# Mixture-of-experts passes of a two-layer block: the next pass's first gate and up products issued before the down products

## The chip, the cores and the metric

The kernel runs on one core of one Trainium2 chip. The metric is device time in microseconds (us) of one execution, the median of three runs. TensorE (PE in the profile) multiplies, with its weight loads shown apart (PEld); VectorE (DVE) and ScalarE (ACT) read its results out of PSUM; SyncE (SP) issues the loads of weights.

## The reference

Two blocks of two layers each work on 256 tokens; the second block has 256 context tokens beside them in its first layer. The change lies in the mixture of experts at the end of each layer of the second block, `hier_moe`. Each token goes to two of 32 experts, and for every expert

```
h_e = rows of h that were sent to expert e
y_e = (silu(h_e @ w_gate[e]) * (h_e @ w_up[e])) @ w_down[e]      # 1024 -> 512 -> 1024, f32
out[token] += weight[token, e] * y_e
```

All 32 experts' weights (6 MiB each in f32) are read once per layer. Layer 0 has 512 tokens, layer 1 has 256.

## The kernel before

Each expert has 64 slots for rows. Two experts make a pass: their products lie side by side in the 128 rows of a PSUM bank, the first in rows 0 to 63 and the second in rows 64 to 127. So a layer has 16 passes. Layer 0 has a 17th (`extra`), for one expert with more than 64 rows, which has 128 slots and half the weights. Two passes make a quad of four experts.

A pass has these parts (line numbers of the kernel before):

- `wload` (L1561): SP loads one tile of 1 MiB, [128, 4, 512], into a buffer of one of two pools, `ring` (4 buffers) for every third load and `ring2` for the others. A pass of two experts takes 12 tiles: four for gate and up with the first half of the model width (`kh` 0), four for the second half (`kh` 1), four for down. A buffer comes free when PE has read it.
- gate and up (L1640): 32 matmuls in f32 with 64 columns each, in pairs, one for each expert. In the trace every such f32 matmul is two instructions, so a pass has 64 rows of them. They write the banks `psg` and `psu`.
- `hidden` (L1527 to L1530): tanh on ACT, then two operations on DVE, which end in `eac`.
- `turned` (L1538, L1539): PE turns `eac` with four transposes, ACT copies them out as `eaT`.
- down (L1667): 16 matmuls, 32 rows in the trace, then `split_y` (L1547, L1548), which makes the pair `yh`, `yl`.
- `gather` (L1586, L1587): PE multiplies the tokens with a one-hot matrix (`goh`, made by DVE at L1568), which gives the four experts' rows `xg`. In layer 0 it has four units of 16 instructions for each quad.
- `combine` (L1517, L1518): the way back to the tokens with the transposed one-hot matrix `est`; in layer 0 eight units of four instructions for each quad. DVE reads each unit out (L1520) and adds it to `x` (L1521).
- `scatter_of` (L1602, L1609): four transposes and eight small products, which make `est` and the gate weights `egs`.

`gather` and `combine` are generators. The loop asks them for a unit at fixed places in the program; a scheduler then orders each engine's instructions by what they depend on, so on PE single instructions of one part stand between those of another. PE runs them in the order in which they stand. PSUM has four banks for the products (`acc`) and three for `gather`, `combine`, `turned` and `scatter_of` together (`aux`).

Of the kernel before, what the change touches and what calls it, by code (L numbers as in the profile page):

```python
# [1 line left out]

# [1 line left out]

# [7 lines left out]
F32 = mybir.dt.float32  # L12
F32R = mybir.dt.float32r
BF = mybir.dt.bfloat16
# [1117 lines left out]
        lin_a4(g, oh, ol, w2d, 8, [(512 * c, 512)], (range(half), range(half, len(xt))), ev, before)  # L1132


def open_ring2(g, l):
    g.ring2 = g.moe_st.enter_context(g.tc.tile_pool(name=f"ring2{l}", bufs=(6, 9)[l], side="right"))


def mixer_ab(g, xt):
# [194 lines left out]
def moe(g, l, xt):  # L1334
# [3 lines left out]
    with ExitStack() as st:  # L1338
# [212 lines left out]
        with ExitStack() as s1:  # L1551
# [4 lines left out]
            def wload(name, e, half):  # L1556

                src = h[name][l, e:e + 1] if isinstance(e, int) else h[name][l, ds(e, 1)]
                t = (g.ring2 if loads[0] % 3 else g.ring).tile([P, 4, 512], F32, name="wraw", tag="wraw")
                loads[0] += 1  # L1560
                nc.sync.dma_start(t.rearrange("p k n -> p (k n)"),  # L1561
                                  src.rearrange("e (p k) n -> p (e k n)", p=P)[:, 2048 * half:2048 * half + 2048])
                return t

            def onehot(q, dt):
                oh = pe.tile([P, nt, 4, CAP], dt, name="goh", tag=f"goh{dt}", bufs=2)
                for t in range(nt):
                    nc.vector.tensor_tensor(oh[:, t], posm[:, t, 4 * q:4 * q + 4, None].to_broadcast([P, 4, CAP]),  # L1568
                                            g.iota[:, None, :CAP].to_broadcast([P, 4, CAP]), op=OP.is_equal)
                return oh  # L1570

            def onehot_first(px, dt):
                oh = pe.tile([P, nt, 4, CAP], dt, name="goh", tag=f"goh{dt}", bufs=2)
                for t in range(nt):
                    nc.vector.tensor_scalar(oh[:, t, :2].rearrange("p e c -> p (e c)"), g.iota, px[:, t:t + 1], None, op0=OP.is_equal)
                return oh

            def gather(oh, xg, n=4):
                w = n * CAP
                for fp in range(4):  # L1580
                    ps = g.aux.tile([P, 2, 256], F32, name="auxps", tag="aux")
                    for j in range(2):
                        f = 2 * fp + j
                        for t in range(nt):
                            r = oh[:, t, :n].rearrange("p e c -> p (e c)")
                            nc.tensor.matmul(ps[:, j, :w], hh[:, t, f * P:(f + 1) * P], r, start=(t == 0), stop=False)  # L1586
                            nc.tensor.matmul(ps[:, j, :w], hl[:, t, f * P:(f + 1) * P], r, start=False, stop=(t == nt - 1))  # L1587
                    if fp % 2:
                        nc.scalar.copy(xg[:, 2 * fp:2 * fp + 2, :w], ps[:, :, :w])
                    else:  # L1590
                        nc.vector.tensor_copy(xg[:, 2 * fp:2 * fp + 2, :w], ps[:, :, :w])
                    yield

            def step(units, n):
                for _ in range(n):
                    next(units, None)

            def scatter_of(obp, gates3):

                psb = g.aux.tile([P, nt * P], BF, name="auxpb", tag="aux")  # L1600
                for t in range(nt):
                    nc.tensor.transpose(psb[:, t * P:(t + 1) * P], obp[t], g.identb)  # L1602
                stt = pe.tile([P, nt * P], F32R, name="est", tag="est", bufs=3)
# [12 lines left out]
            xg = pe.tile([P, 8, 4 * CAP], F32, name="xg")  # L1616
            oh = onehot(0, F32R)
            start = gather(oh, xg)
            comb, parts = iter(()), []
            npass = NEXP // 2  # L1620
            first = None
            for pr_ in range(npass + extra):
                q, hp = pr_ // 2, pr_ % 2
                if pr_ < npass:
                    ex = [(slice(64 * e, 64 * e + 64), slice((2 * hp + e) * CAP, (2 * hp + e + 1) * CAP), 2 * pr_ + e) for e in range(2)]
                else:
                    ex = [(slice(0, P), slice(0, P), nc.values_load(tabE0[0:1, 0:1], engines=(mybir.EngineType.SP,), min_val=0, max_val=NEXP - 1))]
                psg = g.acc.tile([P, 512], F32, name="accps", tag="acc")
                psu = g.acc.tile([P, 512], F32, name="accps", tag="acc")
                for kh in range(2):  # L1630
                    step(start, 2)
                    if pr_ == 0 and kh == 0:
                        gates()
                        ob = onehot(0, BF)
                    for nm, pp in (("moe_w_gate", psg), ("moe_w_up", psu)):
                        w = [wload(nm, e, kh) for _, _, e in ex]
                        for k in range(4):
                            K = 4 * kh + k
                            for wt, (rows, cols, _) in zip(w, ex):
                                nc.tensor.matmul(pp[rows], xg[:, K, cols], wt[:, k], start=(K == 0), stop=(K == 7))  # L1640
                        if kh == 0 and pp is psg:
                            if pr_ < npass:
                                obp = [ob[:, t, 2 * hp:2 * hp + 2].rearrange("p e c -> p (e c)") for t in range(nt)]
                                stt, gs = scatter_of(obp, [lambda t, e=e: G3[:, t, e] for _, _, e in ex])
                            else:
                                obp = [ob[:, t, :2].rearrange("p e c -> p (e c)") for t in range(nt)]
                                stt, gs = scatter_of(obp, [lambda t: first[1][:, t]])
                        if hp == 0 and (nt == 4 or pp is psu):
                            step(comb, 2)
                ac = hidden(pe, psg, psu, gs)  # L1650
                turn = iter(())
                if hp == 1 and pr_ + 1 < npass:
                    turn = gather(oh, xg)
                elif pr_ + 1 == npass and extra:
                    turn = gather(oh, xg, 2)
                step(comb, 2 * nt)
                step(turn, 2)
                aT = turned(pe, ac)
                step(turn, 1)
                psd = [g.acc.tile([P, 512], F32, name="accps", tag="acc") for _ in range(2)]  # L1660
                for half in range(2):
                    w = [wload("moe_w_down", e, half) for _, _, e in ex]
                    for kk in range(2):
                        k = 2 * half + kk
                        for c in range(2):
                            for wt, (rows, _, _) in zip(w, ex):
                                nc.tensor.matmul(psd[c][rows], aT[:, k, rows], wt[:, 2 * kk + c], start=(k == 0), stop=(k == 3))  # L1667
                    step(turn, 1)
                parts.append((stt, *split_y(pe, psd, 2)))
                if hp == 1 or pr_ + 2 >= npass + extra:  # L1670
                    for _ in comb:
                        pass
                    comb = combine(pe, parts)
                    parts = []
                if pr_ == 0:
                    first = overflow_table(pe)
                if hp == 0 and pr_ + 2 < npass:
                    oh, ob_next = onehot(q + 1, F32R), onehot(q + 1, BF)
                elif hp == 0 and extra:
                    oh, ob_next = onehot_first(first[0], F32R), onehot_first(first[0], BF)  # L1680
                elif hp == 1:
                    ob = ob_next
            for _ in comb:
                pass

# [150 lines left out]
```

## Time and profile before

| | |
|---|---|
| median of 3 runs | 2850.63 us (2847.06 to 2854.13) |
| the profiled execution | 2851.21 us, span 2849.4 us |
| PE busy | 2679.5 us, 94% |
| PEld, DVE, ACT busy | 1848.9, 1542.7, 1023.0 us |
| bytes read | 690.80 MB, 243 GB/s over the span |
| expert weights read | 390 loads, 1 MiB each |
| layer 0's passes | from 1530.62 to 2099.40 us |
| layer 1's passes | from 2364.79 to 2830.58 us |

PE's busy time is the union of its matmuls' modelled times, so a busy PE can still have matmuls that follow each other more slowly than they could. The start of one row against the start of the next is the better measure, and it is used below.

### The profile page before, as it was taken

The numbers are of one execution on the slowest core, as the hardware profiler recorded it, in microseconds if no ns is written. First come the engines' busy times: TensorE is split into PE (matmuls) and PEld (weight loads), VectorE is DVE, ScalarE is ACT, GpSimd is POOL, SyncE is SP. The second block draws the span as 40 slices with busy tenths as digits, with TensorE's granted clock in tenths as the row PEclk, the third lists the DMA queues.
The fourth block names the chain that finished last, engine by engine and source line by source line (L and its number), as shares of the span: only waits on it lengthen the run. The fifth ranks groups of instructions, "written<-read, shape, count | busy, mean of one in ns | idle before, by whom it ended". The sixth has DMA issues, their size and how long they took to land. (4 is left out here: it accounts for less than half of the span.)

```text
span 2849.4 us, 39299 instructions
## 1 busy us (share of the span) xinstructions
PE 2679.5 (94%) x15773; PEld 1848.9 (65%) x15773; DVE 1542.7 (54%) x2886; ACT 1023.0 (36%) x1809; POOL 131.0 (5%) x172
## 2 busy tenths in 40 slices
PE   7999999999999999979998999999979998999997
PEld 5989889978899989766565444444458554433332
DVE  6767768857677678565755333332263555222223
ACT  4556546545575456343741110100022441111111
POOL 0000000000000000021011000000000330000000
PEclk9999999999999999989997999999989899999999
DMA  6544466664454576642155999999933357999996
GB/s 222 184 148 161 145 231 212 220 228 157 159 175 142 184 266 207 200 151 74 33 216 211 391 360 368 368 369 369 368 125 132 102 211 297 420 420 420 420 420 265
DMA packets 207434, 694.56 MB, mean 244 GB/s; under 512 B 18160, under 2 KB 67760, under 8 KB 151184
## 3 DMA queue, kind: packets, MB, share of 16 engines
q1 hardware_dynamic: 201424, 674.18, 63.4%
q0 software_dynamic: 5824, 17.82, 1.9%
q8 instruction: 126, 2.06, 0.3%
q14 instruction: 60, 0.49, 0.0%
HBM read 690.80 MB, written 1.15 MB: 243 GB/s over the span
## 5 line engine op out<-in xcount | busy, mean ns | idle before, releaser
L159 DVE TENSOR_TENSOR wlo<-wraw,whi 128x1024 fp32r<-128x1024 f32 (+1 forms) x406 | 484.9, 1200 | 221.7 <-ACT whi L158 211.5
L158 ACT CAST whi<-wraw 128x1024 fp32r<-128x1024 f32 (+1 forms) x406 | 418.0, 1035 | 394.2 <-PE accps L245 192.7
L1640 PE MATMUL accps<-wraw,xg 128*64 128x512 f32 x2080 | 506.2, 595 | 0.0
L1640 PEld LDWEIGHTS accps<-wraw,xg 128*64 128x64 f32 x2080 | 160.1, 137 | 289.8 <-issue 287.4
L1667 PE MATMUL accps<-wraw,eaT 128*64 128x512 f32 (+1 forms) x1040 | 276.9, 600 | 3.0 <-ACT eaT L1539 3.0
L244 PE MATMUL accps<-xh,whi 128*128 128x256 f32 x896 | 258.1, 288 | 0.0
L246 PE MATMUL accps<-xh,wlo 128*128 128x256 f32 x896 | 255.6, 285 | 0.0
L245 PE MATMUL accps<-xl,whi 128*128 128x256 f32 x896 | 255.3, 285 | 0.0
L244 PE MATMUL accps<-fxh,whi 128*128 128x256 f32 x704 | 200.5, 285 | 0.5 <-ACT whi L158 0.4
L246 PE MATMUL accps<-fxh,wlo 128*128 128x256 f32 x704 | 199.5, 284 | 0.6 <-DVE wlo L159 0.5
L245 PE MATMUL accps<-fxl,whi 128*128 128x256 f32 x704 | 199.6, 284 | 0.0
L244 PEld LDWEIGHTS accps<-xh,whi 128*128 128x128 f32 x896 | 170.3, 190 | 7.7 <-issue 7.4
L1667 PEld LDWEIGHTS accps<-wraw,eaT 128*64 128x64 f32 (+1 forms) x1040 | 82.3, 137 | 138.6 <-issue 125.7
L1548 DVE TENSOR_TENSOR yl<-accps,yh 128x512 fp32r<-128x512 f32 x66 | 45.5, 691 | 232.8 <-ACT yh L1547 232.6
L245 PEld LDWEIGHTS accps<-xl,whi 128*128 128x128 f32 x896 | 170.1, 190 | 1.2 <-issue 1.0
L246 PEld LDWEIGHTS accps<-xh,wlo 128*128 128x128 f32 x896 | 170.2, 190 | 1.1 <-issue 1.0
L244 PEld LDWEIGHTS accps<-fxh,whi 128*128 128x128 f32 x704 | 135.6, 193 | 6.2 <-issue 5.0
L246 PEld LDWEIGHTS accps<-fxh,wlo 128*128 128x128 f32 x704 | 135.3, 192 | 1.1 <-DVE wlo L159 1.1
L245 PEld LDWEIGHTS accps<-fxl,whi 128*128 128x128 f32 x704 | 135.6, 193 | 0.0
L1527 ACT ACTIVATE eth<-accps 128x512 f32<-128x512 f32 x33 | 19.7, 597 | 321.5 <-PE accps L1640 321.5
L1547 ACT CAST yh<-accps 128x512 fp32r<-128x512 f32 x66 | 38.7, 586 | 216.6 <-PE accps L1667 216.6
L1586 PE MATMUL auxps<-goh,hh 128*128 128x256 f32 (+1 forms) x416 | 109.7, 300 | 3.0 <-issue 3.0
(496 smaller groups left out, 5123.5 us busy)
## 6 DMA issues: line engine op xcount, KB each, us to landing
wraw<-in_moe_w_gate SPq DMA_DIRECT2D x130, 1024.0 KB, 11.4
wraw<-in_moe_w_up SPq DMA_DIRECT2D x130, 1024.0 KB, 12.7
wraw<-in_moe_w_down SPq DMA_DIRECT2D x130, 1024.0 KB, 11.8
wraw<-in_w_in SPq DMA_DIRECT2D x72, 1024.0 KB, 5.0
wraw<-in_w_ada SPq DMA_DIRECT2D x48, 1024.0 KB, 4.9
wraw<-in_ffn_w_up SPq DMA_DIRECT2D x88, 512.0 KB, 5.1
wraw<-in_ffn_w_down SPq DMA_DIRECT2D x20, 1024.0 KB, 5.2
wraw<-in_w_proj_ssd SPq DMA_DIRECT2D x16, 1024.0 KB, 5.1
```

What stands on the lines that cost most here:

```text
L158: nc.scalar.copy(hi[:, :jj, :n], t[:, j:j + jj, :n])
L159: nc.vector.tensor_tensor(lo[:, :jj, :n], t[:, j:j + jj, :n], hi[:, :jj, :n].bitcast(F32), op=OP.subtract)
L244: nc.tensor.matmul(o, wh, a, start=(K == 0 and f % per == 0), stop=False, skip_group_check=True)
L245: nc.tensor.matmul(o, wh, b, start=False, stop=False, skip_group_check=True)
L246: nc.tensor.matmul(o, wl, a, start=False, stop=last, skip_group_check=True)
L1527: nc.scalar.activation(th, psg, AF.Tanh, scale=0.5)
L1547: nc.scalar.copy(yh[:, sl], psd[c])
L1548: nc.vector.tensor_tensor(yl[:, sl], psd[c], yh[:, sl].bitcast(F32), op=OP.subtract)
L1586: nc.tensor.matmul(ps[:, j, :w], hh[:, t, f * P:(f + 1) * P], r, start=(t == 0), stop=False)
L1640: nc.tensor.matmul(pp[rows], xg[:, K, cols], wt[:, k], start=(K == 0), stop=(K == 7))
L1667: nc.tensor.matmul(psd[c][rows], aT[:, k, rows], wt[:, 2 * kk + c], start=(k == 0), stop=(k == 3))
```

## The change

The loop over passes is written anew. Pass p+1's gate and up products with the first half of the width come first, then pass p's `turned`, then one block with up to four units of `combine` and two of `gather` (layer 0), the scatter of pass p+1, then pass p's down products (into the banks that held its gate and up), and last pass p+1's second half of gate and up and its `hidden`. `in_order` chains all PE instructions of the loop in the order of the program text, without a semaphore. `xg` becomes two tiles, one for each half of the width. The one-hot matrices have one buffer instead of two, `est` five instead of three, `yh` and `yl` three instead of two. `ring2` of layer 0 has 5 buffers instead of 6, and loads go to the two pools in proportion to their sizes.

```diff
+@contextmanager
+def in_order(g):
+    tc = g.tc
+    cur = g.nc.cur_bb
+    n = len(cur.bb.instructions)
+    yield
...
+        if k >= n and prev is not None:
+            tc.add_manual_dep(i, prev.name, mybir.DependencyInfo(mybir.DependencyClass.NoSync, mybir.DependencyReason.DATA),
+                              reason="in_order")
+        prev = i
 def open_ring2(g, l):
-    g.ring2 = g.moe_st.enter_context(g.tc.tile_pool(name=f"ring2{l}", bufs=(6, 9)[l], side="right"))
+    g.ring2 = g.moe_st.enter_context(g.tc.tile_pool(name=f"ring2{l}", bufs=(5, 9)[l], side="right"))
+    g.nring2 = (5, 9)[l]
...
-                t = (g.ring2 if loads[0] % 3 else g.ring).tile([P, 4, 512], F32, name="wraw", tag="wraw")
+                t = (g.ring if 4 * loads[0] % (4 + g.nring2) < 4 else g.ring2).tile([P, 4, 512], F32, name="wraw", tag="wraw")
...
+            def gate_up(p, kh):
+                if not kh:
+                    exs[p] = experts(p)
+                    banks[p] = [g.acc.tile([P, 512], F32, name="accps", tag="acc") for _ in range(2)]
+                for nm, pp in zip(("moe_w_gate", "moe_w_up"), banks[p]):
+                    w = [wload(nm, e, kh) for _, _, e in exs[p]]
+                    for k in range(4):
+                        K = 4 * kh + k
+                        for wt, (rows, cols, _) in zip(w, exs[p]):
+                            nc.tensor.matmul(pp[rows], xg[kh][:, k, cols], wt[:, k], start=(K == 0), stop=(K == 7))
+                if kh:
+                    acs[p] = hidden(pe, *banks[p], gsc[p][1])
...
+            gate_up(0, 0)
+            step(turn, 2)
+            scatter(0)
+            oh = onehot(1, F32R)
+            gate_up(0, 1)
+            first = overflow_table(pe)
+            comb, parts, turn = iter(()), [], iter(())
+            with in_order(g):
+                for p in range(passes):
+                    q, hp = p // 2, p % 2
+                    more = p + 1 < passes
+                    if more:
+                        gate_up(p + 1, 0)
+                        aT = turned(pe, acs.pop(p))
+                    if not hp:
+                        turn = gather(oh, xg, 4 if q + 1 < NEXP // 4 else 2) if 2 * q + 2 < passes else iter(())
+                    for u in range(nt // 2):
+                        step(comb, 1)
+                        step(turn, 2 // (nt // 2))
+                        step(comb, 1)
+                    if more:
+                        scatter(p + 1)
+                    else:
+                        for _ in comb:
+                            pass
+                        aT = turned(pe, acs.pop(p))
+                    parts.append((gsc.pop(p)[0], *down(p, aT)))
...
+                    if hp and 2 * q + 4 < passes:
+                        oh = one(q + 2, F32R)
+                    if not hp and 2 * q + 2 < passes:
+                        ob = one(q + 1, BF)
+                    if more:
+                        gate_up(p + 1, 1)
```

Here is how PE's program stands in a quad of layer 0, in the kernel before: from the end of a pass's down products to the end of the next pass's gate and up. One row is one f32 matmul here (two instructions in the trace).

```order
L1667 MATMUL accps<-wraw,eaT 64x512 x8
L1602 LDWEIGHTS goh
L1602 MATMUL auxpb<-identb,goh 128x128
...
L1518 MATMUL auxps<-yl,est 128x512
L1517 MATMUL auxps<-yh,est 128x512
L1640 MATMUL accps<-wraw,xg 64x512
L1518 MATMUL auxps<-yl,est 128x512
...
L1640 MATMUL accps<-wraw,xg 64x512 x7
...
L1640 MATMUL accps<-wraw,xg 64x512 x15
L1538 MATMUL auxps<-cst,eac 128x128 x4
```

The products with weights (64x512) stand in pieces between those of the way back, some of them singly, and the transposes of `eac` follow the last gate and up product at once. The same stretch of the changed kernel, from one pass's down products to the next pass's (`xg_15661` and `xg_15662` are the two halves of `xg`):

```order
L1670 MATMUL accps<-wraw,eaT 64x512 x16
L1657 MATMUL accps<-wraw,xg_15662 64x512 x16
L1657 MATMUL accps<-wraw,xg_15661 64x512 x16
L1557 MATMUL auxps<-cst,eac 128x128 x4
L1536 MATMUL auxps<-yh,est 128x512
...
L1605 MATMUL auxps<-goh,hh 128x256
...
L1621 MATMUL auxpb<-identb,goh 128x128
...
L1628 MATMUL adaps<-gate_15412,goh 128x3
L1670 MATMUL accps<-wraw,eaT 64x512 x16
```

All 48 products with weights of a pass now stand together, and 16 of them stand between the end of gate and up of a pass (`xg_15662`) and the transposes of its `eac`.

SP's loads of one pass in the steady part, before:

```order
L1561 DMA wraw<-in_moe_w_gate 128x2048 x2
L1561 DMA wraw<-in_moe_w_up 128x2048 x2
L1561 DMA wraw<-in_moe_w_gate 128x2048 x2
L1561 DMA wraw<-in_moe_w_up 128x2048 x2
L1561 DMA wraw<-in_moe_w_down 128x2048 x4
```

And in the changed kernel, where the first four are those of pass p+1, the next four those of pass p, the last four those of pass p+1:

```order
L1580 DMA wraw<-in_moe_w_gate 128x2048 x2
L1580 DMA wraw<-in_moe_w_up 128x2048 x2
L1580 DMA wraw<-in_moe_w_down 128x2048 x4
L1580 DMA wraw<-in_moe_w_gate 128x2048 x2
L1580 DMA wraw<-in_moe_w_up 128x2048 x2
```

The number of loads and their sizes are the same; the four loads of down have moved ahead of the second half of the next pass's gate and up.

## Rows read from the trace of the kernel before

**Rows 1.** Busy times by stretch: steady part of layer 0's passes, then layer 1's.

```profile
core 0: us, PE busy (x) PEld busy (x) DVE busy (x) ACT busy (x) POOL busy (x), PEclk, DMA share, GB/s
1640.00:2000.00 360.00, 346.42 (x1687) 154.14 (x1683) 110.54 (x200) 36.44 (x65) 0.00 (x0) 1.00 0.92 367
2400.00:2700.00 300.00, 289.53 (x1341) 119.39 (x1338) 76.31 (x133) 33.75 (x62) 0.00 (x0) 1.00 1.01 420
```

**Rows 2.** Timeline of ACT: the tanh of passes two apart, layer 0, layer 1.

```profile
1708.48 0.60 ACT L1527 ACTIVATE eth<-accps 128x512 f32<-128x512 f32 x1 [2.85 <-PE accps L1640]
...
1777.22 0.60 ACT L1527 ACTIVATE eth<-accps 128x512 f32<-128x512 f32 x1 [2.85 <-PE accps L1640]
...
2519.37 0.60 ACT L1527 ACTIVATE eth<-accps 128x512 f32<-128x512 f32 x1 [2.85 <-PE accps L1640]
...
2579.01 0.60 ACT L1527 ACTIVATE eth<-accps 128x512 f32<-128x512 f32 x1 [2.85 <-PE accps L1640]
```

**Rows 3.** Timeline of PE in layer 0: start us, us, what, [idle before].

```profile
1713.13 0.63 PE L1538 MATMUL auxps<-cst,eac 128*128 128x128 f32 x4 [1.28 <-DVE eac L1530]
1713.51 0.36 PE L1586 MATMUL auxps<-goh,hh 128*128 128x256 f32 x1
...
1715.50 3.65 PE L1667 MATMUL accps<-wraw,eaT 128*64 128x512 f32 x16
1719.09 0.39 PE L1586 MATMUL auxps<-goh,hh 128*128 128x256 f32 x1
...
1726.86 0.50 PE L1518 MATMUL auxps<-yl,est 128*128 128x512 f32 x1
...
1729.35 3.65 PE L1640 MATMUL accps<-wraw,xg 128*64 128x512 f32 x14
...
1733.59 1.07 PE L1640 MATMUL accps<-wraw,xg 128*64 128x512 f32 x2
1734.59 0.50 PE L1518 MATMUL auxps<-yl,est 128*128 128x512 f32 x1
```

**Rows 4.** Who waited for whom, PE in layer 0's passes: total us, times, longest.

```profile
PE auxps L1538 <- DVE eac L1530: 17.0, 14, 1.3
```

**Rows 5.** Timeline of PE in layer 1: a whole run of gate and up.

```profile
2390.97 13.90 PE L1640 MATMUL accps<-wraw,xg 128*64 128x512 f32 x64
2404.80 0.39 PE L1586 MATMUL auxps<-goh,hh 128*128 128x256 f32 x1
```

**Rows 6.** Timeline of PE: layer 0's first weight products, and what follows the last.

```profile
1530.62 3.65 PE L1640 MATMUL accps<-wraw,xg 128*64 128x512 f32 x16
1534.21 0.40 PE L1602 MATMUL auxpb<-identb,goh 128*128 128x128 bf16 x4
...
1534.71 0.65 PE L1640 MATMUL accps<-wraw,xg 128*64 128x512 f32 x2
...
2099.40 0.50 PE L1517 MATMUL auxps<-yh,est 128*128 128x512 f32 x1
```

**Rows 7.** Timeline of layer 1's ends: SP's first refill; PE's last down products.

```profile
2368.47 0.33 SPq L1561 DMA_DIRECT2D wraw<-in_moe_w_gate  x1
...
2823.51 7.14 PE L1667 MATMUL accps<-wraw,eaT 128*64 128x512 f32 x32 [0.73 <-ACT eaT L1539]
2830.58 0.51 PE L1517 MATMUL auxps<-yh,est 128*128 128x512 f32 x1
```

**Rows 8.** DMA from 2760 to 2849 us, GB/s in 40 equal slices.

```profile
GB/s 420 420 423 420 416 423 409 416 423 423 423 420 420 420 420 420 427 420 420 423 416 409 420 431 409 390 243 59 4 0 0 0 151 92 0 4 35 276 160 0
```

**Rows 9.** DMA issues of the page: KB each, median us to landing.

```profile
wraw<-in_w_in SPq DMA_DIRECT2D x72, 1024.0 KB, 5.0
```

**Rows 10.** Timeline of DVE at the end of layer 0: units of the way back.

```profile
2103.41 1.28 DVE L1520 TENSOR_TENSOR cmt<-auxps,g2r 128x512 f32<-128x512 f32 x2
...
2105.81 1.28 DVE L1520 TENSOR_TENSOR cmt<-auxps,g2r 128x512 f32<-128x512 f32 x2
```

**Rows 11.** Busy times by stretch (columns of rows 1): PE with idle time, and after it.

```profile
938.00:941.30 3.30, 1.88 (x16) 1.67 (x16) 1.29 (x2) 0.00 (x0) 1.61 (x1) 1.00 0.14 17
941.30:944.70 3.40, 3.40 (x18) 3.40 (x18) 1.22 (x1) 0.00 (x0) 0.00 (x0) 0.50 0.78 292
```

More of the change, by code (lines that the diff above doesn't have):

```diff
@@ L1 @@
-from contextlib import ExitStack
+from contextlib import ExitStack, contextmanager
 import numpy as np
@@ L1132, in out_proj @@
         lin_a4(g, oh, ol, w2d, 8, [(512 * c, 512)], (range(half), range(half, len(xt))), ev, before)
+@contextmanager
[4 more added lines that the diff above has]
+    yield
+    assert g.nc.cur_bb is cur
+    prev = None
+    for k, i in enumerate(cur.bb.instructions):
+        if i.engine != mybir.EngineType.PE:
+            continue
+        if k >= n and prev is not None:
+            tc.add_manual_dep(i, prev.name, mybir.DependencyInfo(mybir.DependencyClass.NoSync, mybir.DependencyReason.DATA),
+                              reason="in_order")
+        prev = i
 def open_ring2(g, l):
-    g.ring2 = g.moe_st.enter_context(g.tc.tile_pool(name=f"ring2{l}", bufs=(6, 9)[l], side="right"))
+    g.ring2 = g.moe_st.enter_context(g.tc.tile_pool(name=f"ring2{l}", bufs=(5, 9)[l], side="right"))
+    g.nring2 = (5, 9)[l]
 def mixer_ab(g, xt):
@@ L1565, in onehot @@
             def onehot(q, dt):
-                oh = pe.tile([P, nt, 4, CAP], dt, name="goh", tag=f"goh{dt}", bufs=2)
+                oh = pe.tile([P, nt, 4, CAP], dt, name="goh", tag=f"goh{dt}", bufs=1)
                 for t in range(nt):
@@ L1572, in onehot_first @@
             def onehot_first(px, dt):
-                oh = pe.tile([P, nt, 4, CAP], dt, name="goh", tag=f"goh{dt}", bufs=2)
+                oh = pe.tile([P, nt, 4, CAP], dt, name="goh", tag=f"goh{dt}", bufs=1)
                 for t in range(nt):
@@ L1588, in gather @@
                     if fp % 2:
-                        nc.scalar.copy(xg[:, 2 * fp:2 * fp + 2, :w], ps[:, :, :w])
+                        nc.scalar.copy(xg[fp // 2][:, 2:4, :w], ps[:, :, :w])
                     else:
-                        nc.vector.tensor_copy(xg[:, 2 * fp:2 * fp + 2, :w], ps[:, :, :w])
+                        nc.vector.tensor_copy(xg[fp // 2][:, 0:2, :w], ps[:, :, :w])
                     yield
@@ L1602, in scatter_of @@
                     nc.tensor.transpose(psb[:, t * P:(t + 1) * P], obp[t], g.identb)
-                stt = pe.tile([P, nt * P], F32R, name="est", tag="est", bufs=3)
+                stt = pe.tile([P, nt * P], F32R, name="est", tag="est", bufs=5)
                 nc.scalar.copy(stt, psb)
@@ L1614, in scatter_of @@
                 return stt, gs
[L1616 to L1619, printed above, removed]
+            xg = [pe.tile([P, 4, 4 * CAP], F32, name=f"xg{i}") for i in range(2)]
             npass = NEXP // 2
[L1621 to L1660, printed above, removed]
@@ new lines, in moe, with experts @@
+            passes = npass + extra
+            def experts(p):
+                if p < npass:
+                    hp = p % 2
+                    return [(slice(64 * e, 64 * e + 64), slice((2 * hp + e) * CAP, (2 * hp + e + 1) * CAP), 2 * p + e) for e in range(2)]
+                return [(slice(0, P), slice(0, P), nc.values_load(tabE0[0:1, 0:1], engines=(mybir.EngineType.SP,), min_val=0, max_val=NEXP - 1))]
+            exs, banks, gsc, acs = {}, {}, {}, {}
+            def gate_up(p, kh):
[10 more added lines that the diff above has]
+                    acs[p] = hidden(pe, *banks[p], gsc[p][1])
@@ L1661, in moe, with down @@
+            def down(p, aT):
+                psd = banks.pop(p)
                 for half in range(2):
-                    w = [wload("moe_w_down", e, half) for _, _, e in ex]
+                    w = [wload("moe_w_down", e, half) for _, _, e in exs[p]]
                     for kk in range(2):
@@ L1665, in moe @@
                         for c in range(2):
-                            for wt, (rows, _, _) in zip(w, ex):
+                            for wt, (rows, _, _) in zip(w, exs[p]):
                                 nc.tensor.matmul(psd[c][rows], aT[:, k, rows], wt[:, 2 * kk + c], start=(k == 0), stop=(k == 3))
[L1668 to L1682, printed above, removed]
+                return split_y(pe, psd, 3)
+            def scatter(p):
+                if p < npass:
+                    hp = p % 2
+                    obp = [ob[:, t, 2 * hp:2 * hp + 2].rearrange("p e c -> p (e c)") for t in range(nt)]
+                    gsc[p] = scatter_of(obp, [lambda t, e=e: G3[:, t, 2 * p + e] for e in range(2)])
+                else:
+                    obp = [ob[:, t, :2].rearrange("p e c -> p (e c)") for t in range(nt)]
+                    gsc[p] = scatter_of(obp, [lambda t: first[1][:, t]])
@@ new lines, in one @@
+            def one(q, dt):
+                return onehot(q, dt) if q < NEXP // 4 else onehot_first(first[0], dt)
+            oh = onehot(0, F32R)
+            turn = gather(oh, xg)
+            step(turn, 2)
+            gates()
+            ob = onehot(0, BF)
+            gate_up(0, 0)
+            step(turn, 2)
+            scatter(0)
[3 more added lines that the diff above has]
+            comb, parts, turn = iter(()), [], iter(())
@@ new lines, in moe @@
+            with in_order(g):
[13 more added lines that the diff above has]
+                        scatter(p + 1)
+                    else:
+                        for _ in comb:
+                            pass
+                        aT = turned(pe, acs.pop(p))
+                    parts.append((gsc.pop(p)[0], *down(p, aT)))
+                    if hp or p + 2 >= passes:
+                        for _ in comb:
+                            pass
+                        comb = combine(pe, parts)
+                        parts = []
+                    if hp and 2 * q + 4 < passes:
[4 more added lines that the diff above has]
+                        gate_up(p + 1, 1)
```

## The prediction

> **What bounds the kernel now.** I read the page first: PE is busy for 94% of the span, but that is a union of modelled times, so I went on to the busy times by stretch. There the two expert stages differ [rows 1]: in layer 1 the DMA engines are full (share 1.01, 420 GB/s), in layer 0 they are not (0.92, 367 GB/s), while PE runs at its full clock (1.00) in both. The reader is to see that layer 1 is at the limit of its loads and layer 0 has 13% to gain before it meets that limit. Next I took the length of a pass, from tanh to tanh two passes apart [rows 2]: layer 0 takes 68.74 us for two passes (34.4 each), layer 1 takes 59.64 (29.8 each). Two passes load 24 tiles, so a tile takes DMA 59.64/24 = 2.485 us where it is full. Since a pass of layer 0 loads the same 12 tiles, its floor by DMA is 29.8 us as well. What takes the other 4.6 us is read from the timeline of PE and from the waits: in layer 0 no wait on a load shows, and the one repeated wait is that of the transposes for `eac` [rows 4].
>
> **What PE needs for a pass of layer 0 without interruptions.** A whole run of 64 rows of gate and up, with the turn to another shape at its end, takes 13.83 us [rows 5]; the 96 of a pass take 1.5 times that, 20.75. Sixteen rows of gather take 1.99 us (1713.51 to 1715.50) [rows 3]; a pass has 32 on average, 4.0. Ten rows of the way back, with the turn at the end, take 2.49 (1726.86 to 1729.35) [rows 3]; 16 for each pass give 4.0. Scatter and the turn behind it take 0.50 (1534.21 to 1534.71) [rows 6], the four transposes of `eac` 0.38 [rows 3]. Sum: 29.6 us. The quad of layer 0 that I read (68.74) has 9.5 us more than twice that, and I find them in three places:
> - the transposes wait. They follow the last gate and up product, and `hidden` has to run first: PE is idle for 1.28 us before them [rows 3], 14 times in this stage with 17.0 us in all [rows 4], and the modelled ends of its matmuls hide some 0.3 us more. About 3 us a quad.
> - pairs are broken. Two rows of gate and up that stand alone take 1.00 us (1733.59 to 1734.59) [rows 3], and the 14 others of that pair of tiles still take as long as a whole run of 16, which is 3.59 [rows 6]. In the quad from 1705 to 1774 this happens four times, once with four rows (1.86 us): together 4.9 us.
> - turns. A piece of 16 takes 3.59, where 16 in a long run take 13.83/4 = 3.46, and the first row of another shape starts about 0.1 us late. A dozen more turns cost some 2.5 us.
>
> These add to 10.4, a little over the 9.5, so I keep 29.6 as PE's need.
>
> **The change part by part.** *One block.* The order of PE shows all products with weights of a pass in one run and one block of everything else: one turn each way. That takes away the broken pairs and most turns.
>
> *Sixteen products between `hidden` and its transposes.* They take 6.9 us (two pairs of tiles at 3.46), `hidden` needs about 2 us after the last product, so the wait goes to nothing. The copy of `eaT` (0.6 us on ACT) lies under the block. If that cover were gone, 1.6 us a pass would come back, 26 us in layer 0.
>
> *The chain of PE's order* has no semaphore. It costs nothing by itself, but an instruction that waits now holds everything behind it: in the block, a unit of the way back that finds no `aux` bank holds the down products. DVE frees these banks at 1.2 us a unit (two units in 2.40 us [rows 10]) against 1.0 on PE. A block has four such units and two of gather, so DVE needs 4 x 1.2 + 0.7 = 5.5 us in a block of 8.9: no wait by these numbers. From below the cost is 0; from above it is four units that each wait for one more pair of DVE operations, 2.4 us a pass. I take 0, since the sum leaves 3.4 us free.
>
> *One buffer for each one-hot matrix.* DVE must wait for the block that reads it, and then has more than 20 us of weight products before the next block; 0, or 1.4 us a quad if that cover were gone.
>
> *Down in the banks of gate and up.* These were read out by `hidden` a whole half of gate and up earlier: 0.
>
> *Loads.* Number and size are the same, SP only takes them in another order. Layer 0 could run nine loads ahead before (six buffers took two loads of three) and can run nine ahead now. While a block runs, 8.9 us, no buffer comes free; DMA can use 8.9/2.485 = 3.6 tiles in that time. During the 20.75 us of weight products twelve buffers come free and DMA lands 20.75/2.485 = 8.35 tiles, so at least 3.65 are on their way when a block starts. That is just enough, with nothing to spare. From below this costs 0, from above half a tile a pass, 1.2 us. Layer 1 could run twelve ahead (four buffers took one load of three) and can run 13 ahead now: one tile less to load after the stage has started, 2.5 us.
>
> **The sum, layer 0.** From the first weight product to the end of the last down products it takes 2099.40 - 1530.62 = 568.8 us [rows 6]. After: 17 runs of 20.75 = 352.8 (the 17th pass has one expert with 128 columns and as long a run); gather, seven quads, half of the first and the 17th pass's at 8.0 = 68; the way back, eight quads at 8.0 = 64; scatter and transposes 17 x 0.9 = 15; 3 us for the overflow table's transposes at the start, where PE waits for DVE, and for `eaT` at the end. Together 503. DMA alone would need, for the 189 tiles that are not loaded ahead, 470 us: it is done earlier, but in the steady part its 29.8 us are a little over PE's 29.6, which I count as 2 us. So 505, a gain of 64.
>
> **Layer 1.** In the steady part PE needs 20.75 + 2.0 + 2.0 + 0.6 = 25.4 us and DMA 29.8: it stays at the limit of the loads, now with PE waiting. The gain is at the ends. SP issues the first refill at 2368.47 [rows 7], a single tile lands 5.0 us later [rows 9], and 178 more follow at 2.485: the last lands at 2815.8, before it was about 2819 [rows 8]. Before, PE had fallen behind: its last down products started at 2823.51 and ended at 2830.58 [rows 7]. Now the last half of gate and up ends 3.5 us after its last tile (2805.9 + 3.5), then `hidden`, the transposes and the copy take 3.2, and the two halves of down end at 2819.6. Gain 11; I count 10.
>
> The profiled execution took 2851.21 us, so 2851.2 - 64 - 10 = 2777. The median of the runs lies 0.6 under that execution, hence 2776.
>
> **The rivals.** *PE stays the slower side in layer 0.* The fixed order meets late banks, or the nine-deep ring runs dry: 1 to 2.5 us a pass come back, 16 to 40 us, 2792 to 2816. For it: two limits, 29.6 and 29.8, so close together, and 3.65 tiles against 3.6. Against it: in a steady row the run of products refills what the block drains (8.35 and 3.56 tiles against twelve, with nine ahead at the start), and DVE has 3.4 us to spare in each block.
>
> *Layer 0 can't load faster than it does.* Layer 0 reads at 367 GB/s. If that were a limit of its own, only layer 1's 10 us would remain: 2841. Against it: the same loads run at 420 in layer 1 [rows 1]. The Trainium skill (DMA: Bandwidth & Descriptors, Specifications) gives about 358 GB/s for each core from HBM; by that the change could do nothing here, but rows 1 show 420 for 300 us, and the measurement decides.
>
> *The clock falls in layer 1.* This is the side on which the change loses. PE will wait there for 4.4 of 29.8 us in each pass. Where PE was busy for 1.88 of 3.30 us, the granted clock then stood at 0.50, that is at 1.2 instead of 2.4 GHz [rows 11]. With a share f of the time at half the clock a pass takes 25.4/(1 - f/2): nothing is lost up to f = 0.3, the whole gain is lost at f = 0.52 (34.4 us a pass), and with f = 2/3 it is 38 us, 2909 in all. Against it: a pair of tiles lands every 5.0 us and keeps PE for 3.5, so single waits are at most 1.5 us, no longer than those for `eac` now, under which the clock stayed at 1.00 [rows 1, 3]; and at half the clock PE has no waits, which brings the clock back. [...]
>
> That the change isn't made as described is no rival: the order of PE shows it.
>
> **How the numbers follow.** The forecast as worked out, 2764 to 2792: 0.70. PE slower in layer 0, 2792 to 2816: 0.15. No gain in layer 0, about 2841: 0.04. The clock in layer 1: 0.05, most of it slower than before. More gain than worked out, since the three places add to 0.9 us a quad more than I use and the ends may shrink further, under 2764: 0.06. The range 2764 to 2806 takes in the first case and most of the second. A change of 0.3%, 8.6 us, is about what a measurement of this kernel can tell from none. The first two cases and the last are faster, 0.91; no gain in layer 0 is at the edge, same 0.05; the clock slower 0.04.
>
> **What would show it.** In layer 0 two passes should take 59.6 to 60.5 us from tanh to tanh, DMA should be at 410 GB/s or more, and the waits of the transposes for `eac` should be gone but for the last pass. Layer 1 should still take 59.6 for two passes, with waits of PE on loads that weren't there, a clock of 1.00, and 11 us less behind the last tile. The prediction is wrong if layer 0's quad stays over 62 us, if PE waits inside the block, or if the clock of layer 1 falls.

## The result and the profile after

The changed kernel takes 2781.9 us (median of 4 runs, 2777.5 to 2789.6), the kernel before 2850.3 in the same series: a ratio of 0.976, 95% interval 0.974 to 0.979. Forecast were 2776 and a range of 2764 to 2806. The profiled execution took 2780.57 us, with a span of 2778.8.

The busy times by stretch, with the columns of [rows 1], show the two expert stages of the changed kernel:

```profile
1640.00:2000.00 360.00, 357.83 (x1901) 181.53 (x1900) 129.07 (x228) 42.09 (x72) 0.00 (x0) 1.00 1.01 420
2330.00:2630.00 300.00, 274.56 (x1346) 111.24 (x1342) 77.22 (x137) 34.81 (x63) 0.00 (x0) 1.00 1.01 420
```

Layer 0 now reads 420 GB/s instead of 367, as layer 1 did and does; the clock is 1.00 (2.4 GHz) in both. Timeline of ACT, the tanh of passes two apart (as [rows 2]), for layer 0, for layer 1, and for one place in layer 1 that is longer:

```profile
1774.23 0.60 ACT L1546 ACTIVATE eth<-accps 128x512 f32<-128x512 f32 x1 [2.85 <-PE accps L1657]
...
1833.98 0.60 ACT L1546 ACTIVATE eth<-accps 128x512 f32<-128x512 f32 x1 [2.85 <-PE accps L1657]
...
2443.97 0.60 ACT L1546 ACTIVATE eth<-accps 128x512 f32<-128x512 f32 x1 [2.85 <-PE accps L1657]
...
2503.76 0.60 ACT L1546 ACTIVATE eth<-accps 128x512 f32<-128x512 f32 x1 [2.85 <-PE accps L1657]
...
2593.45 0.60 ACT L1546 ACTIVATE eth<-accps 128x512 f32<-128x512 f32 x1 [2.85 <-PE accps L1657]
...
2654.80 0.60 ACT L1546 ACTIVATE eth<-accps 128x512 f32<-128x512 f32 x1 [2.85 <-PE accps L1657]
```

Two passes take 59.75 us in layer 0 (68.74 before) and 59.79 in layer 1 (59.64 before). The last pair of rows is 61.35 apart; layer 0 has two such places. The timeline of PE for one pass of layer 0 answers to [rows 3]:

```profile
1770.55 14.51 PE L1657 MATMUL accps<-wraw,xg 128*64 128x512 f32 x64
1784.99 0.66 PE L1557 MATMUL auxps<-cst,eac 128*128 128x128 f32 x4
1785.41 0.48 PE L1536 MATMUL auxps<-yh,est 128*128 128x512 f32 x1
...
1793.50 7.09 PE L1670 MATMUL accps<-wraw,eaT 128*64 128x512 f32 x32
1800.41 6.18 PE L1657 MATMUL accps<-wraw,xg 128*64 128x512 f32 x28
```

The transposes of `eac` start without idle time, and the block from them to the down products lasts 8.51 us. The 64 rows of gate and up take 14.44 us instead of the 13.83 of [rows 5]. I read this as waits for their tiles that lie mostly behind modelled ends, so that only a little of it is seen as idle time; with fewer bytes to load, below, the 13.83 are back. PE's waits, first in layer 0 from 1560 to 2000 us, where this is the only one listed, then the two largest in layer 1:

```profile
PE accps L1657 <- DMA wraw<-in_moe_w_up: 3.5, 3, 1.3
...
PE accps L1657 <- DMA wraw<-in_moe_w_up: 22.1, 23, 1.3
PE accps L1657 <- DMA wraw<-in_moe_w_gate: 15.1, 12, 1.3
```

The 14 waits for `eac` of [rows 4] are gone. Last, the ends of both stages, in the timelines of PE and of SP (as [rows 6, 7]):

```profile
1523.26 7.09 PE L1657 MATMUL accps<-wraw,xg 128*64 128x512 f32 x32
...
2033.49 0.49 PE L1536 MATMUL auxps<-yh,est 128*128 128x512 f32 x1
...
2298.82 3.54 PE L1657 MATMUL accps<-wraw,xg 128*64 128x512 f32 x14
...
2302.81 0.80 SPq L1580 DMA_DIRECT2D wraw<-in_moe_w_down  x2
...
2749.32 0.51 PE L1536 MATMUL auxps<-yh,est 128*128 128x512 f32 x1
...
2753.13 7.09 PE L1670 MATMUL accps<-wraw,eaT 128*64 128x512 f32 x32 [0.73 <-ACT eaT L1558]
2760.15 0.50 PE L1536 MATMUL auxps<-yh,est 128*128 128x512 f32 x1
```

Layer 0 takes 2033.49 - 1523.26 = 510.2 us (568.8 before), layer 1 takes 2760.15 - 2298.82 = 461.3 (465.8 before, with 2364.79 from the table of before and 2830.58 from [rows 7]). That is 63.1 us less. The two profiled executions differ by 70.6; of the rest, 7.4 us lie ahead of 1523.26, where PE's program is the same in both.

### The profile page after: what moved, and what is told of

It reads as the page before. It is cut to its first block, busy times and chain, and to the rows that moved or that the text cites. A ratio compares the mean times of both kernels' runs of the same rounds, so it can differ in the third digit from the quotient of the medians.

```text
span 2778.8 us, 39439 instructions
## 1 busy us (share of the span) xinstructions
PE 2604.0 (94%) x15773; PEld 1840.4 (66%) x15773; DVE 1542.2 (55%) x2878; ACT 1024.1 (37%) x1809; POOL 131.0 (5%) x172
## 5 line engine op out<-in xcount | busy, mean ns | idle before, releaser
L1657 PE MATMUL accps<-wraw,xg 128*64 128x512 f32 x2080 | 489.0, 595 | 40.8 <-DMA wraw<-in_moe_w_up 25.6
L1670 PE MATMUL accps<-wraw,eaT 128*64 128x512 f32 (+1 forms) x1040 | 234.2, 595 | 1.5 <-ACT eaT L1558 1.5
L1539 DVE TENSOR_TENSOR cmt<-auxps,g2r 128x512 f32<-128x512 f32 x108 | 73.6, 688 | 263.8 <-PE auxps L1537 263.2
L1558 ACT COPY eaT<-auxps 128x512 f32<-128x512 f32 x33 | 19.4, 586 | 408.7 <-PE auxps L1557 408.7
L1670 PEld LDWEIGHTS accps<-wraw,eaT 128*64 128x64 f32 (+1 forms) x1040 | 74.6, 137 | 133.2 <-issue 129.3
```

Source lines behind the costliest of these rows:

```text
L1539: nc.vector.tensor_tensor(tm, ps, g2r[m][:, sl], op=OP.mult)
L1558: nc.scalar.copy(aT, ps)
L1657: nc.tensor.matmul(pp[rows], xg[kh][:, k, cols], wt[:, k], start=(K == 0), stop=(K == 7))
```

## The experiments

All were compared with the kernel before on their chip (2850.6 us there for the first four, 2849.5 for the others). The table gives each one's median, then from its profiled execution the start of the first product with weights, the length of each expert stage, and two passes in their steady part, all read as above.

| kernel | median | first product at | layer 0 | layer 1 | two passes, layer 0 | layer 1 |
|---|---|---|---|---|---|---|
| before | 2850.3 | 1530.6 | 568.8 | 465.8 | 68.74 | 59.64 |
| changed | 2781.9 | 1523.3 | 510.2 | 461.3 | 59.75 | 59.79 |
| without the chain | 2841.1 | 1524.7 | 559.0 | 466.7 | 67.12 | 59.84 |
| transposes first | 2796.4 | 1529.0 | 521.5 | 459.7 | 61.85 | 59.91 |
| old loop, chained | 2794.2 | 1529.7 | 517.6 | 461.5 | 60.97 | |
| fewer bytes | 2716.0 | 1524.3 | 497.0 | 404.5 | 58.52 | 50.48 |
| seven loads ahead | 2806.1 | 1529.6 | 530.7 | 460.0 | 62 to 64 | |
| 17th pass in the middle | 2776.6 | 1519.2 | 507.8 | 463.0 | | |
| its control | 2789.3 | 1535.6 | 509.6 | 463.0 | 59.75 | |
| half the products in layer 1 | 2771.4 (one run) | 1522.6 | 509.8 | 455.2 | | 58.1 to 62.2 |

"First product at" is worth a look before the other columns: the same code ahead of the stages ends between 1519.2 and 1535.6 us. That is as large as the differences between several of the medians, so the stages are what is compared below.

**Without the chain.**

```diff
-            with in_order(g):
+            if True:
```

> The changed kernel without the chain of PE's order, all else as it is (same loop, banks, pools, loads). The scheduler then puts one product of the next pass, not sixteen, ahead of the transposes of eac, and cuts the 1560 products with weights of both layers into 139 pieces instead of 40, 41 of them of one or two products. Theory (PE's order is what set the time of layer 0): the wait for eac comes back with 1.4 us a pass, two broken pairs and two or three turns add 2.4 + 0.6, so a pass of layer 0 needs 34.0 us on PE against 29.85 by loads; 16 x 4.15 = 66 us more, 2835 to 2855 in all. Layer 1 needs 25.4 + 4.4 = 29.8, level with its loads, so nothing more there. Rival (the new buffers, the halves of xg and the order in which loads are issued gave the gain): 2782.

Measured: 2841.1 us, ratio to before 0.997 (0.996 to 0.998). Timeline of PE in layer 0:

```profile
1771.44 0.63 PE L1557 MATMUL auxps<-cst,eac 128*128 128x128 f32 x4 [1.27 <-DVE eac L1549]
...
1773.86 3.65 PE L1657 MATMUL accps<-wraw,xg 128*64 128x512 f32 x14
...
1778.11 1.07 PE L1657 MATMUL accps<-wraw,xg 128*64 128x512 f32 x2
...
1781.65 3.65 PE L1657 MATMUL accps<-wraw,xg 128*64 128x512 f32 x14
```

The wait for `eac` is back with 1.27 us; two rows alone take 1.07, and the 14 that are left of their pair of tiles take 3.65, as long as 16. Two passes take 67.12 us (68 expected, 34.0 a pass). The new loop, buffers and loads alone are worth 568.8 - 559.0 = 9.8 us of layer 0. Layer 1 is 5.4 us longer than in the changed kernel, where nothing was expected. Its passes in the steady part are as long; but its last tile lands 11.2 us before the stage ends, against 4.5 in the changed kernel.

**The old loop, chained.** The kernel before with nothing of the change but `in_order`:

```diff
-            for pr_ in range(npass + extra):
...
+            with in_order(g):
+                for pr_ in range(npass + extra):
```

> The kernel before with only the chain of PE's order around its old loop: no product of the next pass ahead of the transposes, units of gather and way back at their old places, but no longer mixed with single products (110 pieces of 4 products or more, where before there were 156 with 47 of one or two). Theory (broken pairs and turns were the larger part of what PE lost): the pairs stay whole, about half of the waits for eac and some turns stay, 62.5 us for two passes of layer 0 against 68.7 before and 59.7 after the change: 2797 to 2808. Rival (only the pipelining of one pass into the next counts): 2840 to 2850. Second rival (the old places make instructions queue behind a late bank in the chain): over 2850.

Measured: 2794.2 us, ratio 0.980 (0.977 to 0.983). Timeline of ACT in layer 0, and PE's waits for `eac` in the whole stage:

```profile
1754.81 0.60 ACT L1545 ACTIVATE eth<-accps 128x512 f32<-128x512 f32 x1 [6.64 <-PE accps L1659]
...
1815.78 0.60 ACT L1545 ACTIVATE eth<-accps 128x512 f32<-128x512 f32 x1 [6.64 <-PE accps L1659]
```

```profile
PE auxps L1556 <- DVE eac L1548: 1.2, 1, 1.2
```

60.97 us for two passes is less than the 62.5 expected, and the median lies under the 2797 to 2808 expected, because I counted on half of the waits for `eac` to stay. In the text of the old loop units of the way back and of gather stand between `hidden` and the transposes; it was the scheduler that had pulled the transposes ahead of them. So the chain mends the broken pairs and the waits, and brings 51.2 of the 58.6 us of layer 0. The rest of the change, on top of it, brings the other 7.4: the pipelining, with its buffers and its order of loads. The rival, that only the pipelining counts, has fallen, and so has the one of instructions held up behind a late bank.

**The transposes first.** The chain and the block stay, the cover ahead of the transposes goes:

```diff
+                        aT = turned(pe, acs.pop(p))
                         gate_up(p + 1, 0)
-                        aT = turned(pe, acs.pop(p))
```

> The changed kernel with the transposes of pass p ahead of the first half of gate and up of pass p+1 instead of behind it; the chain and the one block stay otherwise. Theory (PE and loads are level in layer 0, so a wait of PE shows at once, and layer 1 hides it under its loads): the wait for eac takes 1.3 us in the profile and 0.3 behind modelled ends, one more turn 0.2, so PE's need in layer 0 goes from 29.6 to 31.4 us a pass against 29.85 now: 16 x 1.55 = 25 us more, 2800 to 2812; layer 1's PE need is 27.2 against 29.8, no change. Rival (the loads alone set both layers): 2782, no change.

Measured: 2796.4 us, ratio 0.981 (0.979 to 0.983). PE's waits in layer 0, and two neighbouring passes in its timeline:

```profile
PE auxps L1557 <- DVE eac L1549: 18.9, 15, 1.3
```

```profile
1757.98 0.63 PE L1557 MATMUL auxps<-cst,eac 128*128 128x128 f32 x4 [1.31 <-DVE eac L1549]
1758.54 7.09 PE L1657 MATMUL accps<-wraw,xg 128*64 128x512 f32 x32
...
1788.84 0.66 PE L1557 MATMUL auxps<-cst,eac 128*128 128x128 f32 x4 [1.22 <-DVE eac L1549]
```

Layer 0 is 11.3 us longer, layer 1 isn't: there PE waits for loads anyway. The rival (loads alone set both) is out for layer 0. But 25 us were expected, and 2800 to 2812 in all; two passes take 61.85 where I had 62.8. The next run tells why.

**Fewer bytes.** Of each down tile only half is loaded and used twice:

```diff
-                nc.sync.dma_start(t.rearrange("p k n -> p (k n)"),
-                                  src.rearrange("e (p k) n -> p (e k n)", p=P)[:, 2048 * half:2048 * half + 2048])
+                n = 1024 if name == "moe_w_down" else 2048
+                nc.sync.dma_start(t.rearrange("p k n -> p (k n)")[:, :n],
+                                  src.rearrange("e (p k) n -> p (e k n)", p=P)[:, 2048 * half:2048 * half + n])
...
-                                nc.tensor.matmul(psd[c][rows], aT[:, k, rows], wt[:, 2 * kk + c], start=(k == 0), stop=(k == 3))
+                                nc.tensor.matmul(psd[c][rows], aT[:, k, rows], wt[:, c], start=(k == 0), stop=(k == 3))
```

> The changed kernel, but of each tile of the down weights only the first half is loaded, and its columns are used twice; so half of the down weights is left out of the result. A pass loads 10 MiB instead of 12: 24.9 us at the speed now measured. PE does the same work. Theory (loads are now the limit in both layers, with PE close behind in layer 0): layer 0 falls to PE's need, 29.6 us a pass, 3 to 8 us in all, and layer 1 to PE's need of 25.4 us a pass, 66 us in all: 2704 to 2714. Rival (what is left in layer 0 and 1 is PE's order and its waits on banks, not loads): 2775 to 2782. Rival (the loads are limited by their number, each tile costs 2.5 us whatever its size): 2782.

Measured: 2716.0 us, 2 us over the range expected, ratio 0.954 (0.952 to 0.956). Stretches as above, the tanh in both layers, and one pass of layer 0 on PE:

```profile
1640.00:2000.00 360.00, 360.00 (x1948) 176.30 (x1946) 131.70 (x231) 43.69 (x75) 0.00 (x0) 1.00 0.87 344
2330.00:2630.00 300.00, 300.00 (x1550) 126.92 (x1548) 86.75 (x152) 39.71 (x72) 0.00 (x0) 1.00 1.02 418
```

```profile
1797.17 0.60 ACT L1546 ACTIVATE eth<-accps 128x512 f32<-128x512 f32 x1 [2.85 <-PE accps L1658]
...
1855.69 0.60 ACT L1546 ACTIVATE eth<-accps 128x512 f32<-128x512 f32 x1 [2.85 <-PE accps L1658]
...
2424.00 0.60 ACT L1546 ACTIVATE eth<-accps 128x512 f32<-128x512 f32 x1 [2.85 <-PE accps L1658]
...
2474.48 0.60 ACT L1546 ACTIVATE eth<-accps 128x512 f32<-128x512 f32 x1 [2.85 <-PE accps L1658]
```

```profile
1764.23 13.90 PE L1658 MATMUL accps<-wraw,xg 128*64 128x512 f32 x64
1778.06 0.66 PE L1557 MATMUL auxps<-cst,eac 128*128 128x128 f32 x4
...
1786.58 7.09 PE L1671 MATMUL accps<-wraw,eaT 128*64 128x512 f32 x32
```

In layer 0 the DMA engines are no longer full (0.87), and PE is. Its own need of a pass is therefore 58.52/2 = 29.26 us: 13.83 for gate and up, 8.52 for the block, 6.92 for down. Loads cost the changed kernel 510.2 - 497.0 = 13.2 us in layer 0 and 56.8 in layer 1, where I had expected 3 to 8 and 66. In layer 1 the DMA engines are full again at 50.48 us for two passes (1.02, 418 GB/s), and PE is busy throughout, so I take that as no more than a bound from above on PE's need there: 25.24 us a pass. The rivals (no load limit; a price for each tile whatever its size) are out. With 29.26 in place of 29.6 the run before reads rightly: 61.85/2 - 29.26 = 1.67 us for the uncovered transposes, where I had 1.8.

**Seven loads ahead.**

```diff
-    g.nring2 = (5, 9)[l]
+    g.nring2 = (3, 9)[l]
```

and the same in the pool's `bufs`.

> The changed kernel with three buffers instead of five in the second pool of layer 0, so that seven loads run ahead instead of nine; layer 1 is as it was. Theory (nine are just enough, as a block takes 8.9 us and two tiles are always in flight for 5.0 us after their issue): with seven, a block finds too few tiles landed or too few buffers free; 1 to 2 us a pass, and two tiles less loaded ahead of the stage (5 us): 18 to 35 us more, 2800 to 2817. Rival (the number of buffers counts only as a lead at the start): 5 us more, 2787.

Measured: 2806.1 us, ratio 0.985 (0.983 to 0.987). PE's waits in layer 0:

```profile
PE accps L1657 <- DMA wraw<-in_moe_w_up: 15.5, 15, 1.6
PE accps L1657 <- DMA wraw<-in_moe_w_gate: 2.2, 4, 1.3
```

Layer 0 is 20.4 us longer, of which the lead at the start explains 5 by the estimate above: the rest goes with waits of PE for a tile, 19 in 17 passes. With nine the DMA engines are full (420 GB/s), so a longer lead would have little to add; seven are not enough.

**The 17th pass in the middle.** Since layer 0's last pass has half the loads and as much work for PE, I tried it behind the eighth pass, against a control. In both the loop over passes is rewritten so that it walks over a list of quads; they differ in one line:

```diff
-                quads.insert(8, [npass])
+                quads.insert(4, [npass])
```

> The changed kernel with layer 0's seventeenth pass (the one for the expert with more than 64 rows) put in the middle, behind the eighth pass, instead of at the end; the same work otherwise. Theory (in layer 0 the loads are now the slower side in the 16 regular passes, 29.87 us against PE's 29.26 in the run with fewer bytes, while the seventeenth has half the loads and as much work of PE, and stands at the end, where nothing is left to load): in the middle it lets the loads catch up by about 5 us, and the stage ends some 14 us behind its last load instead of 27; 5 to 11 us less than the control in the same call, in which the pass stands at the end: 2770 to 2778. Rival (the gap between loads and PE is not what costs, or the longer block around the pass eats it): no difference from the control within 3 us.

The control:

> The control: the same rewritten loop with the seventeenth pass at the end, where it stands in the changed kernel; PE's order in both layers' passes is that of the changed kernel. Both theories: 2778 to 2786, the time of the changed kernel.

Measured: 2776.6 us against 2789.3 for the control (2778 to 2786 expected), ratios to before 0.976 (0.973 to 0.979) and 0.979 (0.977 to 0.981). The medians look like the theory. The stages don't: layer 0 takes 507.8 against 509.6 us, and layer 1 the same. The spans of the profiled executions differ by 16.6 us, and the first product starts 16.4 us earlier in the one than in the other (timeline of PE):

```profile
1519.19 2.37 PE L1657 MATMUL accps<-wraw,xg 128*64 128x512 f32 x10
```

```profile
1535.59 2.80 PE L1657 MATMUL accps<-wraw,xg 128*64 128x512 f32 x12
```

PE's program up to there is the same, and the granted clock is not: here from 600 to 700 us (columns of [rows 1]), in the kernel with the pass in the middle and in the control:

```profile
600.00:700.00 100.00, 95.60 (x586) 77.99 (x585) 75.84 (x208) 51.27 (x79) 1.11 (x2) 1.00 0.58 192
```

```profile
600.00:700.00 100.00, 96.30 (x518) 77.25 (x517) 67.58 (x189) 44.02 (x67) 1.11 (x2) 0.93 0.57 193
```

The instructions that the first runs in these 100 us take 5.7 us more in the control. The five executions of the kernel with the pass in the middle show it too: they run from 2771.9 us at a mean granted clock of 0.977 to 2791.1 us at 0.968. So most of the 12.8 us between the medians says nothing of the moved pass, and the rival holds: 1.8 us instead of 5 to 11. The stretch around the moved pass shows where the rest went, in the kernel with the pass in the middle and in the control:

```profile
1770.00:1830.00 60.00, 60.00 (x294) 31.11 (x292) 26.47 (x46) 6.75 (x12) 0.00 (x0) 1.00 0.87 345
```

```profile
1770.00:1830.00 60.00, 60.00 (x322) 29.46 (x321) 21.90 (x38) 7.05 (x12) 0.00 (x0) 1.00 1.01 420
```

The DMA engines are idle there for 13% of the time. The block with the gathers of two quads is long, PE is busy throughout, and SP waits up to 6.9 us for a buffer that gate and up read, against 2.6 in the control. What the loads could have caught up, they lose. Neither this nor any other full version that I ran is measurably better than the changed kernel.

**Half the products in layer 1.** Every second product is left out there (`if l and k % 2: continue` in `gate_up`, `range(1 if l else 2)` in `down`), and every load is made.

> The changed kernel, but layer 1 leaves out every second product with weights (half of the sums of gate, up and down); its loads are all made. PE then needs about 15 us of the 29.85 of a pass, and waits for loads half of the time instead of 15%. Theory (layer 1 is limited by loads alone): its passes still take 59.7 to 59.8 us in pairs, and the whole 2776 to 2784. The rival of the forecast (PE's clock falls when it waits for loads) shows here, if anywhere, as a granted clock under 1.00 in layer 1; at 0.50 throughout PE would need 29.8 us a pass, level with the loads, and the time would be up to 10 us longer. With the clock at 1.00 here too, the kernel is far from where the clock would fall.

Measured: 2771.4 us in one run. Stretches of layer 1:

```profile
2330.00:2630.00 300.00, 218.95 (x813) 80.48 (x812) 71.98 (x126) 33.08 (x60) 0.00 (x0) 0.95 1.01 420
2440.00:2455.00 15.00, 12.17 (x40) 4.79 (x38) 2.23 (x3) 0.59 (x1) 0.00 (x0) 0.81 1.01 420
```

Two passes take between 58.1 and 62.2 us here, but the pace is the same: from the fifth tanh of the stage to the last it is 330.4 us, in the changed kernel 331.0. Of the 6.1 us less of this stage, 5.3 lie ahead of the fifth tanh; that start, which I had not counted on, is the larger part of what puts the time under the 2776 to 2784 expected. With so much waiting the granted clock does fall, to a mean of 0.95, and to 0.81 in the stretch of 15 us shown, that is to 1.2 GHz for a part of it. These eleven passes are not longer for it, as the loads set their pace.

## Why the prediction was right, and where it was off

The forecast of 2776 us lies 0.2% under the median, and for layer 0 its mechanism is the one that the runs show. That it comes so near is in part luck, as the last step below says. By its steps:

- *PE's need of 29.6 us a pass in layer 0.* 29.26. The weights were right (20.75 against 13.83 + 6.92), the block takes 8.52 where I had 8.9. Over the stage PE alone needs 497.0 us, not 503.
- *Three places that lose 9.5 us a quad.* Before, two passes took 68.74 - 58.52 = 10.2 more than PE's need. Waits for `eac`: 61.85 - 58.52 = 3.3 with the cover gone (about 3 forecast). What the old loop still lost when chained: 60.97 - 58.52 = 2.45 (2.5 forecast for the turns). That isn't all turns: PE waits there for the copies of `eaT` too, 6.8 us in the stage (before, 1.7), or 0.8 a quad. Broken pairs: by difference 4.5 (4.9 forecast). Neither the turns nor the broken pairs were measured by themselves.
- *No wait in the block, nothing for the single one-hot buffers and the shared banks.* The one wait of PE listed from 1560 to 2000 us is for loads.
- *Nine tiles are just enough.* With nine the DMA engines are full in the steady part, and seven cost 20.4 us. Before, it was one more than I counted: the trace has ten loads issued ahead of the first product.
- *Loads a little over PE, counted as 2 us.* This is the step that failed in layer 0: 13.2. From the fourth tanh on the passes go at the pace of the loads, 29.88 against 29.26, and 12 of them make 7.4 us; two of these are 1.55 us longer still, 3.1; and the pass before them takes 31.88, 2.6 more, where the loads have not yet caught up. PE's need being 6 us lower than I had it hid half of this, so the stage came out at 510.2 instead of 505.
- *10 us at the ends of layer 1.* 4.5. From the first refill to the end I had 2819.6 - 2368.47 = 451.1 us, and it took 2760.15 - 2302.81 = 457.3. Three readings fail here. Gate and up ended 446.5 us after the first refill (440.9 forecast), and the rest took 10.8 (10.2): the term of 178 loads at 2.485 us was too small, as two tiles are 1.55 us late and the second tile comes 3.6 us after the first. The tile less to load isn't there: in the traces thirteen loads of layer 1 are issued ahead of the first refill in both kernels, and from the landing of that refill to the landing of the last tile it takes 448 us in both. And "11 us less behind the last tile" rests on an end of the loads before that I took from the rates of [rows 8] as about 2819. In the trace the last tile lands at 2823.18, 7.4 us before the stage ends; in the changed kernel at 2755.65, 4.5 before the end. So 2.9 us went there and not 8, and the other 1.5 lie ahead of the first refill's landing.
- *The sum.* 63 us of the 74 forecast came from the stages: by them alone the profiled execution would have taken 2788. It is nearer to the forecast since the stretch ahead of the stages happened to be 7.4 us shorter in it. That is luck. The granted clock from 1300 to 1400 us is 1.00 in this execution and 0.97 in the one before, with the same program.

Of the rivals, slow loads are refuted: layer 0 reads at 420 GB/s. The Trainium skill (DMA: Bandwidth & Descriptors, Specifications) has about 358 GB/s for a core; both layers of this trace stand above it. PE as the slower side is refuted by the run with fewer bytes. The clock stayed at 1.00 in layer 1 with single waits of at most 1.3 us. A fall shows only with half of the products left out, and there it did not change the pace. The Trainium skill (TensorE: Matmul & The Clock Gate, HAM oscillation) describes a fall of the clock in a loop whose waits for loads are longer than its runs of products. Layer 1 of the changed kernel is not such a loop: two tiles keep PE for 3.5 of the 5.0 us in which they land.

What I had not weighed was which of the two halves of the change does the work: the chain of PE's order alone brings 51.2 us of layer 0, the new loop without it 9.8.

## What to carry to other kernels

If a scheduler cuts long runs of small matmuls into pieces, first fix the order of that engine as the program text has it, and measure; here this was seven eighths of layer 0's gain, ahead of any pipelining. When one engine is sped up, work out the next limit as closely as the first: of two limits within 1% of each other (29.6 and 29.8 us here) the one that was to cost 2 us cost 13, once its own irregularities were counted. Compare stages, not totals, when the part of the program that is not under test varies by more than the effect.

## What the runs showed of the hardware

A stream of loads that fills the DMA engines is not quite even. Twice in each stage of the changed kernel a tile lands 4.0 to 4.2 us after the one before, instead of 2.5. Three of the four times two passes then take 61.3 us instead of 59.8, as in the rows at 2593.45 and 2654.80 above; the fourth falls in the start of layer 1, where the passes are not yet even. The DMA engines are not idle then: this is the DMA view of the four microseconds from 2379 to 2383 us, at that fourth place:

```profile
DMA packets 228, 1.65 MB, mean 414 GB/s; under 512 B 27, under 2 KB 27, under 8 KB 27
...
q1 hardware_dynamic: 227, 1.64, 99.3%
q8 instruction: 1, 0.02, 1.7%
```

A fetch of instructions stands among the packets, and one does at each of the other three places too. But so it does in most stretches of 30 us without such a delay (there are 16 on this queue in layer 1's passes). Whether the late tiles wait for such a fetch no run here tells; it stays open.
